# A two-layer fp32 decoder trunk on one core: norm tails moved to VectorE, softmax statistics moved to ScalarE's DMA queue, and a re-ordered start

## The chip, the cores and the metric

The kernel runs on one core of one Trainium2 chip. A core has five engines that run beside each other, each with its own in-order instruction stream: TensorE (PE; its weight loads are listed as PEld), VectorE (DVE), ScalarE (ACT), GpSimd (POOL) and SyncE (SP). Sixteen DMA engines move data. The metric is the device time of one launch in microseconds (us), the median of several runs. The profile is of one execution and has its own time.

## The reference

One sequence of 1024 positions, model width 1024, two layers, all fp32:

```python
for i in range(DEPTH):                       # DEPTH = 2
    j = i // N_MIXERS
    if i % N_MIXERS == 0:
        y = dilated_attention_mixer(x, attn_w_in[j], attn_w_out[j])
    else:
        y = hgrn2_mixer(x, hgrn_w_in[j], hgrn_w_out[j], hgrn_norm_g[j], lbs[i])
    x = layer_norm(DEEPNORM_ALPHA * x + y, ln_mix_g[i], ln_mix_b[i])
    y = squared_relu_mlp(x, ffn_w_up[i], ffn_w_down[i])     # width 4096
    x = layer_norm(DEEPNORM_ALPHA * x + y, ln_ffn_g[i], ln_ffn_b[i])
```

The attention has 16 heads of 64 and three dilations, 1, 4 and 16. Each query sees itself and the 128 keys behind it in its residue class. The three outputs of a head are mixed per position by a softmax over their log-sum-exps:

```python
for g, (window, dilation) in enumerate(((128, 1), (512, 4), (2048, 16))):
    o, lse = dilated_window_attention(rotary(q[g]), rotary(k[g]), v[g], window, dilation)
    outs.append(o); lses.append(lse)
wts = softmax(stack(lses), axis=0)
o = einsum('gbsh,gbshe->bshe', wts, stack(outs))  @ w_out
```

The second layer's mixer is a gated linear recurrence (HGRN2) of 8 heads of 128, computed in chunks of 64 positions, with a norm per head.

## The kernel before, in words

Every fp32 product is done as three matmuls on split operands: a value is cut into a high part in the format fp32r (a ScalarE copy) and a low part (a VectorE difference), and high x high, low x high and high x low are added in PSUM. `split` does the cut; its two lines appear in the profile as L137 (ScalarE) and L138 (VectorE).

**Attention, projections.** The input projection uses seven products of combined blocks instead of eight. `make_T(i)` forms the combined and split input block of product kind `i` (the blocks T1 to T4 are differences, L351); blocks are kept in DRAM (`keep_T`) and loaded again by `get_T` (L394). Weights are loaded by `load_w`, combined by VectorE (`wc`, L423 to L429), and split by `split_w_` (ScalarE, high half, L432) and `low_w` (VectorE, low half, L440) into a tile `H`. `product(n)` runs 12 matmuls of 128x512 (L669 to L671) for the product `n`; its result is copied by ScalarE or added by VectorE into `e`, `vp` and `vT` (L692 to L704). There are 12 groups of 21 products; a group serves two units, a unit being one pair of heads with one dilation, so there are 8 x 3 = 24 units.

**Attention, units.** The rest of a unit (rotary, scores L502, exponentials L516, transposes of the probabilities `ppt` L526, their copies `pts` L529, the products with v into bank `o` L541, and the copies `og` L549 and L552) is cut into pieces. They are put behind the products of the next group through the table `fill`.

**Mixing of the dilations.** For each unit `combine_tr` transposes the statistics, copies them to `sr` (ScalarE, L569), stores `sr` to the DRAM tensor `mdram` (L572), and loads it in another layout into `ml` (L578 for dilation 1, L581 for the others). After the third unit of a pair `combine` works out the weights `fh` and `fl` (high and low, L612 and L614) and writes them by six DMAs into the rows of `frow` (L619). `combine_mul` spreads them with a matmul into `fb` (L629) and multiplies and adds (L630 to L633). All DMAs of the kernel are issued by SP.

**The end of attention.** The last group's units have no products behind which they could stand; the lists `tail` and `mine` place their pieces between the matmuls of the output projection (`rows`, L183 to L185, with the split inputs `aoh`, `aol` and weights `woh`, `wol`).

**Norms.** `ln_math` (L193 to L214) makes the statistics on VectorE and ScalarE, subtracts the mean and multiplies by the gain in one VectorE pass (L199), scales by the inverse deviation on ScalarE (L213) and adds the bias on GpSimd (L214). The result `z` is transposed by TensorE (`lnpt`, L223) and split again (L233, L234) as input of the next part. The last norm of the kernel writes its output instead (L207 to L212).

**Feed-forward and recurrence.** `ffn` runs an up projection (L1116 to L1118) and a down projection (L1264 to L1268). `hgrn` runs the recurrence by heads: the pieces of head `hd` are put into a list `pend` that runs beside the projections of the next head (L171 to L173).

**Order.** The instructions of an engine run in the order of its stream. A scheduler sets that order, except where `in_order` pins a stretch to the order in which the code is written: TensorE and VectorE in attention; TensorE, VectorE and SP in the feed-forward part. ScalarE's order is the scheduler's everywhere.

Of the kernel before, what the change touches and what calls it, by code (L numbers as in the profile page):

```python
# [22 lines left out]
DIL = (1, 4, 16)  # L23
# [12 lines left out]
SPILL = (6, 5)  # L36
NKA = (6, 7)
EARLY = (2, 0)
NAHEAD = 8
NSTAY = 4  # L40
LATE = 2
# [21 lines left out]
def trunk_kernel(  # L63
# [62 lines left out]
    nc.scalar.preload_act_table_set("natural_log_exp_and_others")  # L126
    ident = cp.tile([P, P], F32, name="ident")
    make_identity(nc, ident)
    eps_ln = cp.tile([P, 1], F32, name="eps_ln")
    nc.gpsimd.memset(eps_ln, LN_EPS)  # L130
    eps_rms = cp.tile([P, 1], F32, name="eps_rms")
# [4 lines left out]
    def split(raw, hi, lo):  # L136
        act(hi, raw, AF.Copy)  # L137
        nc.vector.tensor_sub(lo, raw, hi.bitcast(F32))  # L138
# [54 lines left out]
    def ln_math(z, gB, bB, store=None):  # L193
        st = small([P, 2, 6], "lnst")
        for i in range(2):
            nc.vector.bn_stats(st[:, i], z[:, i * 512:(i + 1) * 512])
        mv = small([P, 2], "lnmv")
        nc.vector.bn_aggr(mv, st)
        nc.vector.scalar_tensor_tensor(z, z, mv[:, 0:1], gB, op0=ALU.subtract, op1=ALU.mult)  # L199
        w = small([P, 4], "lnw")  # L200
        act(w[:, 0:1], mv[:, 1:2], AF.Ln, bias=eps_ln)
        act(w[:, 1:2], w[:, 0:1], AF.Exp, scale=-0.5)
        r = w[:, 1:2]
        nc.vector.tensor_scalar(w[:, 2:3], mv[:, 1:2], LN_EPS, r, op0=ALU.add, op1=ALU.mult)
        nc.vector.tensor_scalar(w[:, 2:3], w[:, 2:3], r, -0.5, op0=ALU.mult, op1=ALU.mult)
        nc.vector.tensor_scalar(w[:, 3:4], w[:, 2:3], 1.5, r, op0=ALU.add, op1=ALU.mult)
# [6 lines left out]
        act(z, z, AF.Copy, scale=w[:, 3:4])  # L213
        nc.gpsimd.tensor_add(z, z, bB)  # L214

    def z_tr(z):

# [104 lines left out]
    def attention(pre, hc):  # L322
# [30 lines left out]
        def make_T(i):  # L353
            v, g = nc.vector, nc.gpsimd
            if i == 6:
                combine_x("T1", xr["12"], xr["11"], v)
                combine_x("T2", xr["22"], xc["T1"], v)
            elif i == 7:
                combine_x("T3", xr["22"], xr["12"], v)
            elif i == 4:  # L360
                combine_x("T4", xr["21"], xc["T2"], v)
            src = {1: "11", 2: "21", 6: "T2", 7: "T3", 3: "22", 5: "T1", 4: "T4"}[i]
            src = xc.pop(src) if src == "T3" or src == "T4" else xc[src] if src in xc else xr[src]
            hi = [U("xh", F32R) for _ in range(2)]
            lo = [U("xl", F32R) for _ in range(2)]
            for q in range(2):
                if i == 2:
                    for c in (L, R):
                        split(src[q][:, c], hi[q][:, c], lo[q][:, c])
                else:  # L370
                    split(src[q], hi[q], lo[q])
            return hi, lo
# [64 lines left out]
        def low_w(n):  # L437
            if n in lows:
                v = nc.vector
                v.tensor_sub(H[n][:, R], lows.pop(n), H[n][:, L].bitcast(F32))  # L440
# [123 lines left out]
        def combine_tr(pr, g, slot, ml):  # L564
            pt = bank("pt", "mpt")
            nc.tensor.transpose(pt[:, 0:P], allS, ident)
            q = slice(slot * 32, slot * 32 + 32)
            sr = small([P, P], "sr", 2)
            act(sr[q], pt[q, 0:P], AF.Copy)  # L569
            yield  # L570
            md = mdram[pr, g]
            nc.sync.dma_start(md.rearrange("w h (b q) -> (w h b) q", q=P), sr[q])  # L572
            yield

            d = DIL[g]
            for w in range(2):
                if d == 1:
                    nc.sync.dma_start(ml[:, w, 0, :], md[w].rearrange("h (i n) -> (h i) n", n=P))  # L578
                else:
                    for h in range(2):  # L580
                        nc.sync.dma_start(  # L581
                            ml[8 * h:8 * h + 8, w, g, :].rearrange("i (r n) -> i r n", r=d),
                            md[w, h].rearrange("(r i n) -> i r n", r=d, i=8))
            yield

        def combine(pr, ml):
# [27 lines left out]
            v.tensor_sub(fl, l, fh.bitcast(F32))  # L614
            yield
            for g in range(NG):
                for i, f in enumerate((fh, fl)):
                    r = 4 * g + 2 * i
                    nc.sync.dma_start(frow[r:r + 2, :].bitcast(F32).rearrange("h (i t) -> h i t", t=P),  # L619
                                      f[:, g, :].bitcast(F32))  # L620
            yield

        def combine_mul(pr, og, hb):
# [124 lines left out]
        for c in (R, L):  # L748
# [3 lines left out]
            if c == R:  # L752
                for q in range(2):
                    load_x("11", q)
        get_T(0, 0)
        for b in ("12", "22"):
            for q in range(2):
                load_x(b, q)
        for n in range(LOADW):
            load_w(n)  # L760
        for n in range(SPLITW):
            split_w_(n)
            if n <= SPLITW - 2:
                low_w(n)
        for n in range(len(seq)):
            gi, i, j = seq[n]
            load_w(n + LOADW)
# [14 lines left out]
            if n >= len(seq) - 2 * PREA - 1:  # L782
                next(early, None)
            if n == 0:
                get_T(2, 0)
            if n in KEEP:
                keep_T(KEEP[n])
            product(n)
            for f in fill.pop(n, []):
                f()  # L790
            low_w(n + SPLITW - 2)
            split_w_(n + SPLITW)
            if n % 21 == 14:
                last = gi == len(groups) - 1
                base = n + 7
# [25 lines left out]
        (ra, ca, sa, _), (rb, cb, sb_, mx) = tail  # L821
        done = [f for n in sorted(fill) for f in fill[n]]
        mine = [[ra[0]], [rb[0], rb[1]], [ra[1]], [ca[0], rb[2]], [ca[1]], [cb[0]], [ca[2]], [cb[1]], [ca[3]], [cb[2]],
                [ca[4]] + sa, [cb[3]], [ca[5]], [cb[4]] + sb_, [cb[5]], mx[:1], mx[1:3], mx[3:5], [],
                mx[5:7], mx[7:10], mx[10:]]
        lists = [done[k:k + 1] + (mine[k] if k < len(mine) else []) for k in range(max(len(done), len(mine)))]
        return oN, lists
# [661 lines left out]
    def hgrn(xs, late, consts, pre, gw):  # L1489
# [104 lines left out]
        for hd in range(8):  # L1594
# [64 lines left out]
            oN.append(ond[1, hd] if hd < SPILL[1] else oNt)  # L1659
            new = head_pieces(hd, cur["kd"], cur["kd2"], cur["qd"], e[2], cur["dec"], oNt)  # L1660
            if hd == 0:
                new = [[]] + new
            pend = [(pend[i] if i < len(pend) else []) + (new[i] if i < len(new) else [])
                    for i in range(max(len(new), len(pend)))]
        return oN, pend
# [98 lines left out]
```

## Time and profile before

| | |
|---|---|
| median of 3 runs | 2829.61 us (2828.23 to 2829.97) |
| the profiled execution's own time | 2828.98 us |
| its span, first to last instruction | 2827.2 us |
| TensorE, VectorE, ScalarE, GpSimd busy | 2766.7, 2069.0, 1450.8, 122.9 us |
| GpSimd in the norms' add (L214) | 24 instructions, 58.6 us |
| mean clock granted to TensorE | 0.997 |

The span is the time between the first and the last instruction on the core; the rest of the run's time lies around it. A row of the timeline gives the start, the duration, the engine, the line in the code, what is written from what, the shapes and, in brackets, how long the engine had been idle and what ended that wait. A row with "x2" holds two instructions in a row. In the rows of the waits, the numbers are the total, the count and the longest wait.

### The profile page before, as it was taken

To read this page: it belongs to the slowest core of one execution; us is meant where nothing else is said; L and a number is where in the kernel's file an instruction comes from. 1 tells how busy PE (TensorE), PEld (TensorE's weight loads), DVE (VectorE), ACT (ScalarE), POOL (GpSimd) and SP (SyncE) were. 2 spreads that over 40 slices of the span, in tenths; PEclk is the share of its full clock that TensorE was granted. 3 is DMA by queue.
4 is the path that set the end of the run, shared out by engine and by line. 5 is a ranking of instruction groups with operands and counts; after the bars stand their busy time and mean duration, and the time that the engine had idled before them with its cause. 6 is when DMAs were issued, how large, how long until landed. Compare 5 with 4: busy or idle time off the path is not lost.

```text
span 2827.2 us, 40131 instructions
## 1 busy us (share of the span) xinstructions
PE 2766.7 (98%) x14280; PEld 2229.3 (79%) x14280; DVE 2069.0 (73%) x3830; ACT 1450.8 (51%) x3105; POOL 122.9 (4%) x68
## 2 busy tenths in 40 slices
PE   8999999999999989999999999999999999999998
PEld 6777777777777757888878887788887788878887
DVE  7768777777877767786686876565667787678687
ACT  5455555655555555544454444555553644454443
POOL 0000000000000003100000011111102200000000
PEclk9999999999999999999999999999999999999999
DMA  7766665766666523464494752011132355475654
GB/s 286 255 187 208 191 207 173 217 201 198 201 200 220 168 83 134 146 224 160 152 324 127 260 178 98 8 60 60 61 112 104 128 211 176 154 278 188 221 176 130
DMA packets 204936, 485.27 MB, mean 172 GB/s; under 512 B 29376, under 2 KB 43712, under 8 KB 204736
## 3 DMA queue, kind: packets, MB, share of 16 engines
q1 hardware_dynamic: 204736, 482.72, 51.1%
q8 instruction: 112, 1.84, 0.3%
q14 instruction: 88, 0.72, 0.1%
HBM read 362.82 MB, written 94.24 MB: 162 GB/s over the span
## 4 chain that ended last, share of the span: by engine, by line
PE 90%; DVE 5%; ACT 2%; DMA 1%; issue 1%; POOL 0%; SPq 0%; DVEq 0%; POOLq 0%; ACTq 0%
PE pmm L669 8%; PE pmm L671 8%; PE pmm L670 8%; PE pup L1118 7%; PE pup L1116 7%; PE pup L1117 7%; PE pdy L1268 4%; PE pdy L1264 4%; PE pdy L1267 4%; PE s L502 3%; PE pdx L1267 3%; PE pmm L171 3%; PE pdx L1268 3%; PE pmm L173 3%; PE pdx L1264 3%; PE pmm L172 3%
## 5 line engine op out<-in xcount | busy, mean ns | idle before, releaser
L669 PE MATMUL pmm<-xh,H 128*128 128x512 f32 x1008 | 408.5, 405 | 13.2 <-ACT H L432 9.6
L671 PE MATMUL pmm<-xh,H 128*128 128x512 f32 x1008 | 396.5, 393 | 0.2 <-DVE H L440 0.2
L670 PE MATMUL pmm<-xl,H 128*128 128x512 f32 x1008 | 396.0, 393 | 0.0
L669 PEld LDWEIGHTS pmm<-xh,H 128*128 128x128 f32 x1008 | 190.8, 189 | 54.1 <-ACT H L432 9.6
L671 PEld LDWEIGHTS pmm<-xh,H 128*128 128x128 f32 x1008 | 190.4, 189 | 42.6 <-DVE H L440 1.1
L670 PEld LDWEIGHTS pmm<-xl,H 128*128 128x128 f32 x1008 | 191.1, 190 | 36.6
L516 ACT ACTIVATE p<-p,stats 128x128 f32<-128x128 f32 (+1 forms) x384 | 168.3, 441 | 90.7 <-DVE stats L513 89.3
L1264 PE MATMUL pdy<-dT,dS 128*128 128x512 f32 x512 | 199.2, 389 | 0.0
L1267 PE MATMUL pdy<-dT,dS 128*128 128x512 f32 x512 | 199.2, 389 | 0.0
L1268 PE MATMUL pdy<-dT,dS 128*128 128x512 f32 x512 | 199.2, 389 | 0.0
L513 DVE CUSTOM_DVE_ANT_0 p<-s,mask 128x128 f32<-128x128 f32 (+1 forms) x384 | 113.3, 348 | 66.5 <-PE s L502 56.8
L137 ACT ACTIVATE dS<-dr 128x512 fp32r<-128x512 f32 x192 | 119.5, 622 | 73.1 <-PE pdy L1268 36.6
L171 PE MATMUL pmm<-f0nh,wh 128*128 128x512 f32 x384 | 153.1, 399 | 0.0
L173 PE MATMUL pmm<-f0nh,wl 128*128 128x512 f32 x384 | 150.1, 391 | 1.7 <-DVE wl L138 1.6
L172 PE MATMUL pmm<-f0nl,wh 128*128 128x512 f32 x384 | 149.8, 390 | 0.0
L138 DVE TENSOR_TENSOR dS<-dr,dS 128x512 fp32r<-128x512 f32 x192 | 135.4, 705 | 16.2 <-ACT dS L137 14.3
L214 POOL TENSOR_TENSOR z<-z,bB 128x1024 f32<-128x1024 f32 x24 | 58.6, 2444 | 1673.1 <-ACT z L213 1663.0
L529 ACT ACTIVATE pts<-ppt 128x256 f32<-128x256 f32 (+1 forms) x192 | 85.4, 474 | 61.1 <-PE ppt L526 59.0
L137 ACT ACTIVATE dT<-hold 128x512 fp32r<-128x512 f32 x128 | 80.0, 625 | 69.0 <-DVE hold L1243 28.4
L1077 ACT ACTIVATE H<-wc 128x512 fp32r<-128x512 f32 x128 | 77.2, 625 | 73.3 <-DVE wc L1070 43.9
L1267 PEld LDWEIGHTS pdy<-dT,dS 128*128 128x128 f32 x512 | 96.1, 188 | 20.0
L1268 PEld LDWEIGHTS pdy<-dT,dS 128*128 128x128 f32 x512 | 96.1, 188 | 20.0
(396 smaller groups left out, 6946.6 us busy)
## 6 DMA issues: line engine op xcount, KB each, us to landing
xh<-xtd SPq DMA_DIRECT2D x110, 512.0 KB
xl<-xtd SPq DMA_DIRECT2D x110, 512.0 KB
dr<-hd SPq DMA_DIRECT2D x192, 256.0 KB
dr<-in_w_down_dram SPq DMA_DIRECT2D x128, 256.0 KB
rot<-e SPq DMA_DIRECT2D x192, 128.0 KB
wa<-in_w_up_dram SPq DMA_DIRECT2D x48, 512.0 KB
wb<-in_w_attn_dram SPq DMA_DIRECT2D x36, 512.0 KB
wa<-in_w_attn_dram SPq DMA_DIRECT2D x33, 512.0 KB
```

The source lines that it names most:

```text
L137: act(hi, raw, AF.Copy)
L171: nc.tensor.matmul(o, wh[:, k], xs.h(k), start=k == 0, stop=False)
L172: nc.tensor.matmul(o, wh[:, k], xs.l(k), start=False, stop=False)
L173: nc.tensor.matmul(o, wl[:, k], xs.h(k), start=False, stop=k == NK - 1)
L669: nc.tensor.matmul(o, wh, hi[k // 2][:, c], start=begin and k == 0, stop=False, skip_group_check=True)
L670: nc.tensor.matmul(o, wh, lo[k // 2][:, c], start=False, stop=False, skip_group_check=True)
L671: nc.tensor.matmul(o, wl, hi[k // 2][:, c], start=False, stop=end and k == 3, skip_group_check=True)
L1116: nc.tensor.matmul(o, wh, xf.h(b, k), start=begin and k == 0, stop=False, skip_group_check=True)
L1117: nc.tensor.matmul(o, wh, xf.l(b, k), start=False, stop=False, skip_group_check=True)
L1264: nc.tensor.matmul(o[q], h, T_[:, L], start=begin, stop=False, skip_group_check=True)
L1267: nc.tensor.matmul(o[q], h, T_[:, R], start=False, stop=False, skip_group_check=True)
L1268: nc.tensor.matmul(o[q], l, T_[:, L], start=False, stop=end, skip_group_check=True)
```

## The change

1. **Norms.** The ScalarE pass L213 and the GpSimd add L214 become one VectorE instruction, 24 times.
2. **Statistics.** The store `mdram <- sr` is issued on ScalarE's queue. For dilation 1 there is no trip through DRAM: two DMAs on ScalarE's queue copy `sr` to `ml` directly. Of the six `frow` DMAs of a pair, the three of `fh` go to ScalarE's queue. So ScalarE issues 56 DMAs: 24 for `frow`, 16 stores to `mdram` and 16 direct copies to `ml`.
3. **Last units.** In `mine` the statistics are transposed one slot sooner than they are used.
4. **Warm-up.** 24 transposes of the identity with no use are put at TensorE's start.
5. **Start.** Weight 0 is split between the two halves of the first input block; weights 1 to 5 are split ahead of the next block; a table `FIRSTW` puts off the splits that follow.
6. **First output.** ScalarE follows the written order from product 30 to 33.
7. **Recurrence.** Head 0's pieces start one slot later.

The diff, cut where a part only renames:

```diff
+FIRSTW = {0: (), 1: (), 2: (), 3: ((0, 6),), 4: ((0, 7), (1, 6)), 5: ((0, 8), (1, 7), (0, 9), (1, 8)),
+          6: ((1, 9), (0, 10), (0, 11))}
+NWARM = 24
+FIRSTO = (30, 34)
...
+    warm = bank("s", "warm")
+    for n in range(NWARM):
+        nc.tensor.transpose(warm[:, n % 4 * P:(n % 4 + 1) * P], ident, ident)
...
-        act(z, z, AF.Copy, scale=w[:, 3:4])
-        nc.gpsimd.tensor_add(z, z, bB)
+        nc.vector.scalar_tensor_tensor(z, z, w[:, 3:4], bB, op0=ALU.mult, op1=ALU.add)
...
                 if i == 2:
                     for c in (L, R):
                         split(src[q][:, c], hi[q][:, c], lo[q][:, c])
+                    if q == 0:
+                        between()
...
-            nc.sync.dma_start(md.rearrange("w h (b q) -> (w h b) q", q=P), sr[q])
+            d = DIL[g]
+            if d == 1:
+                for w in range(2):
+                    nc.scalar.dma_start(ml[:, w, 0, :], sr[q0 + 16 * w:q0 + 16 * w + 16])
+            else:
+                nc.scalar.dma_start(md.rearrange("w h (b q) -> (w h b) q", q=P), sr[q0:q0 + 32])
...
-                for i, f in enumerate((fh, fl)):
+                for i, (f, eng) in enumerate(((fh, nc.scalar), (fl, nc.sync))):
...
-        get_T(0, 0)
...
-        for n in range(SPLITW):
+        opT[0] = make_T(2, lambda: (split_w_(0), low_w(0)))
+        for n in range(1, 6):
             split_w_(n)
-            if n <= SPLITW - 2:
-                low_w(n)
+            low_w(n)
+        acts = in_order((mybir.EngineType.Activation,))
...
             if n == 0:
-                get_T(2, 0)
+                combine_T(6)
+            if n == FIRSTO[0]:
+                acts.__enter__()
+            if n == FIRSTO[1]:
+                acts.__exit__()
...
-            low_w(n + SPLITW - 2)
-            split_w_(n + SPLITW)
+            if n in FIRSTW:
+                for f, m in FIRSTW[n]:
+                    (split_w_, low_w)[f](m)
+            else:
+                low_w(n + SPLITW - 2)
+                split_w_(n + SPLITW)
...
-                [ca[4]] + sa, [cb[3]], [ca[5]], [cb[4]] + sb_, [cb[5]], mx[:1], mx[1:3], mx[3:5], [],
+                [ca[4]] + sa[:1], sa[1:] + [cb[3]], [ca[5]], sb_[:1] + [cb[4]], sb_[1:] + [cb[5]], mx[:1], mx[1:3], mx[3:5], [],
...
             if hd == 0:
-                new = [[]] + new
+                new = [[], []] + new
```

How the streams move, at three places. A row is a position in the engine's stream, the line, the operation and what is written from what; line numbers of the changed code are 12 to 14 higher in attention.

VectorE at the start, before. `xl` is the low part of an input block (the full blocks 112 and 114 are those of the second block, xT_171 and xT_172 the block T2), `H` the low half of a weight, `wc` a combined weight:

```order
3 L440 TENSOR_TENSOR H<-wa,H 128x512 x4
4 L138 TENSOR_TENSOR xl<-x_112,xh 128x1024
5 L138 TENSOR_TENSOR xl<-x_114,xh 128x1024
10 L138 TENSOR_TENSOR xl<-xT_171,xh 128x1024
11 L138 TENSOR_TENSOR xl<-xT_172,xh 128x1024
12 L440 TENSOR_TENSOR H<-wa,H 128x512
13 L423 TENSOR_TENSOR wc<-wb 128x512
14 L424 TENSOR_TENSOR wc<-wc,wa 128x512
15 L440 TENSOR_TENSOR H<-wa,H 128x512
16 L423 TENSOR_TENSOR wc<-wb 128x512
```

And after the change:

```order
2 L452 TENSOR_TENSOR H<-wa,H 128x512
3 L145 TENSOR_TENSOR xl<-x_130,xh 128x512 x2
4 L452 TENSOR_TENSOR H<-wa,H 128x512 x5
5 L145 TENSOR_TENSOR xl<-x_137,xh 128x1024
6 L145 TENSOR_TENSOR xl<-x_139,xh 128x1024
11 L145 TENSOR_TENSOR xl<-xT_200,xh 128x1024
12 L145 TENSOR_TENSOR xl<-xT_201,xh 128x1024
13 L708 TENSOR_TENSOR e<-pmm,e 128x512
14 L435 TENSOR_TENSOR wc<-wb 128x512
15 L436 TENSOR_TENSOR wc<-wc,wa 128x512
```

The low halves of weights 4 and 5 moved from behind the blocks T2 to the front, and weight 0's into the middle of the first block.

ScalarE at the first output, before; `og` is the copy of the finished bank `o`, `p,stats` the exponentials:

```order
62 L457 ACTIVATE bsel<-selw 128x384
63 L529 ACTIVATE pts<-ppt 128x256 x2
64 L516 ACTIVATE p,stats<-p,stats 128x128 x4
65 L698 ACTIVATE vp<-pmm 128x512
66 L700 ACTIVATE e<-pmm 128x512
67 L698 ACTIVATE e<-pmm 128x512
68 L552 ACTIVATE og<-o 128x8x64
```

And after:

```order
61 L469 ACTIVATE bsel<-selw 128x384
62 L712 ACTIVATE e<-pmm 128x512
63 L564 ACTIVATE og<-o 128x8x64
64 L528 ACTIVATE p,stats<-p,stats 128x128 x4
65 L541 ACTIVATE pts<-ppt 128x256 x2
66 L444 ACTIVATE H<-wc 128x512
67 L712 ACTIVATE vp<-pmm 128x512
```

The copy `og` moved ahead of the exponentials, the copies `pts` and two copies of projections.

ScalarE at the end of attention, before, where no DMA stands in its stream:

```order
778 L599 ACTIVATE ml<-ml 16x384
779 L137 ACTIVATE aoh<-og 128x512
780 L137 ACTIVATE aoh<-onr 128x512 x2
781 L612 ACTIVATE fh<-ml 16x384
782 L137 ACTIVATE aoh<-onr 128x512
783 L137 ACTIVATE aoh<-og 128x512 x3
```

And after:

```order
821 L613 ACTIVATE ml<-ml 16x384
822 L144 ACTIVATE aoh<-onr 128x512
823 L144 ACTIVATE aoh<-og 128x512
824 L144 ACTIVATE aoh<-onr 128x512
825 L626 ACTIVATE fh<-ml 16x384
826 L633 DMA frow<-fh 2x8x128 x3
827 L144 ACTIVATE aoh<-onr 128x512
828 L144 ACTIVATE aoh<-og 128x512
```

Three issues of `frow` now stand between `fh` and the next split of the projection's input.

More of the change, by code (lines that the diff above doesn't have):

```diff
@@ L351, in combine_x, with combine_T @@
                 eng.tensor_sub(xc[name][q], x[q], y[q])
-        def make_T(i):
-            v, g = nc.vector, nc.gpsimd
+        def combine_T(i):
+            v = nc.vector
             if i == 6:
@@ L361, in make_T @@
                 combine_x("T4", xr["21"], xc["T2"], v)
+        def make_T(i, between=None):
+            if i != 6:
+                combine_T(i)
             src = {1: "11", 2: "21", 6: "T2", 7: "T3", 3: "22", 5: "T1", 4: "T4"}[i]
@@ L566, in combine_tr @@
             nc.tensor.transpose(pt[:, 0:P], allS, ident)
-            q = slice(slot * 32, slot * 32 + 32)
+            q0 = slot * 32
             sr = small([P, P], "sr", 2)
-            act(sr[q], pt[q, 0:P], AF.Copy)
+            act(sr[q0:q0 + 32], pt[q0:q0 + 32, 0:P], AF.Copy)
             yield
             md = mdram[pr, g]
-            nc.sync.dma_start(md.rearrange("w h (b q) -> (w h b) q", q=P), sr[q])
-            yield
[L575 to L579, printed above, removed]
+            d = DIL[g]
[4 more added lines that the diff above has]
+                nc.scalar.dma_start(md.rearrange("w h (b q) -> (w h b) q", q=P), sr[q0:q0 + 32])
+            yield
+            if d > 1:
+                for w in range(2):
                     for h in range(2):
@@ L616, in combine @@
             for g in range(NG):
-                for i, f in enumerate((fh, fl)):
+                for i, (f, eng) in enumerate(((fh, nc.scalar), (fl, nc.sync))):
                     r = 4 * g + 2 * i
-                    nc.sync.dma_start(frow[r:r + 2, :].bitcast(F32).rearrange("h (i t) -> h i t", t=P),
-                                      f[:, g, :].bitcast(F32))
+                    eng.dma_start(frow[r:r + 2, :].bitcast(F32).rearrange("h (i t) -> h i t", t=P),
+                                  f[:, g, :].bitcast(F32))
             yield
```

## The prediction

> **What bounds the kernel now.** I read the engine shares of the page first, then the waits of TensorE (PE), then short pieces of the timeline at the longest of them. The page's engine lines:
>
> ```profile
> PE 2766.7 (98%) x14280; PEld 2229.3 (79%) x14280; DVE 2069.0 (73%) x3830; ACT 1450.8 (51%) x3105; POOL 122.9 (4%) x68
> ```
>
> The reader is to see that TensorE works for 2766.7 of 2827.2 us. Its matmuls are the same after the change, so only its 60.5 us of idle time, and the time in which it works at half clock, can be won. The view of waits says which instruction TensorE waited for (total, times, longest):
>
> ```profile
> PE pmm L669 <- ACT H L432: 9.6, 1, 9.6
> PE pmm L183 <- ACT aoh L137: 4.9, 3, 3.6
> PE pmm L669 <- ACT e L692: 3.6, 1, 3.6
> PE o L541 <- ACT og L552: 3.0, 3, 2.1
> PE fb L629 <- DMA frow<-fh: 2.5, 1, 2.5
> PE lnpt L223 <- issue: 2.3, 3, 1.0
> PE lnpt L223 <- DVE f0nl L234: 2.1, 1, 2.1
> PE pmm L173 <- DVE wl L138: 1.6, 1, 1.6
> PE as L1515 <- DVE qe L1654: 1.4, 1, 1.4
> PE ho L1553 <- DVE stA L1535: 1.3, 1, 1.3
> ```
>
> These ten rows hold 32.3 us, and the change reaches for every one of them. The first three and the clock belong to the start. In the stretches below, the engine columns are busy us and (instructions), then the granted clock.
>
> ```profile
> 9.60:14.10 4.50, 4.50 (x11) 3.43 (x12) 2.38 (x5) 2.04 (x4) 0.00 (x0) 1.00 1.04 406
> 24.40:27.80 3.40, 3.40 (x10) 2.66 (x9) 3.33 (x7) 1.47 (x3) 0.00 (x0) 0.50 1.02 407
> 120.00:123.30 3.30, 3.30 (x10) 2.53 (x9) 0.00 (x0) 1.57 (x4) 0.00 (x0) 0.50 0.77 313
> 23.80:49.80 26.00, 26.00 (x108) 21.38 (x109) 24.84 (x33) 13.86 (x22) 0.00 (x0) 0.93 0.47 184
> ```
>
> A half-clock stretch shows as 10 matmuls in 3.4 us (0.34 us each with the edges; 0.41 in the first row) where 108 in 26.0 us is 0.24 each. Each costs about 1.1 to 2.0 us: 10 x (0.34 - 0.24) = 1.0 at the least, half of 3.4 = 1.7 if the whole stretch is at half. I take 1.7. The first row's clock column reads 1.00, but its 11 matmuls in 4.5 us say half: 11 x (0.41 - 0.23) = 2.0 us lost.
>
> **Part A: warm-up transposes, weight 0 in halves, splits of weights 1 to 5 ahead.** The matmul that waits longest could start before 9.58, but what stands behind it decides the gain: VectorE (DVE).
>
> ```profile
> 1.22 0.29 POOL masks.py:199 TENSOR_SCALAR_AFFINE_SELECT ident<-ident 128x128 f32<-128x128 f32 x1
> L526 PE MATMUL ppt<-ident,p x4: 272/273/327, 96.0 to 96.4; 128*128 128x128 f32 x4
> 15.27 2.36 DVE L138 TENSOR_TENSOR xl<-x,xh 128x1024 fp32r<-128x1024 f32 x2 [0.93 <-ACT xh L137]
> 33.89 1.09 DVE L694 TENSOR_TENSOR vT<-pmm,vp 128x512 f32<-128x512 f32 x1 [0.83 <-PE pmm L671]
> 49.09 0.69 DVE L440 TENSOR_TENSOR H<-wb,H 128x512 fp32r<-128x512 f32 x1
> 50.46 0.39 PE L671 MATMUL pmm<-xh,H 128*128 128x512 f32 x1
> ```
>
> The identity is ready at 1.5 us. Four warm transposes start within 0.4 us, 0.13 each, so 24 at half clock take 24 x 0.26 = 6.2 us and end near 7.8. TensorE was idle until 9.58, so they cost nothing, unless weight 0 is there earlier than 7.8; the first product then starts some 1.8 us sooner. At full clock from there it saves the 2.0 of the first stretch. The wait for e (3.6 us) halves, because the copy of e now stands ahead of the two xh copies of T2 instead of behind them, and its cold stretch of 1.7 goes. Together 1.8 + 2.0 + 1.8 + 1.7 = 7.3 us if TensorE alone decided.
>
> VectorE does not allow it. From 23.8 to 49.8 it is busy 24.84 of 26.00 us, and the low half of weight 12, made from 49.09 to 49.78, is read at 50.46: slack 0.7. VectorE's work to that point is the same after the change. What it gains: two low halves (H4, H5; about 0.6 each at their pitch) go ahead of xl into its idle time, 1.2; the idle 0.83 at 33.89 goes; against it, its first full xl waits for a ScalarE that splits H5 first, so it starts near 15.8 instead of 15.27, -0.5. With the slack, 0.7 + 1.2 + 0.8 - 0.5 = **2.2 us** is how much earlier TensorE can pass that weight. I take 2.2, since the busy share says that VectorE is the bound; ends: 0 (the splits collide with late loads) and 7.3.
>
> **Part B: ScalarE in written order at the first output.**
>
> ```profile
> 109.34 0.66 PE L541 MATMUL o<-pts,vn 128*64 128x128 f32 x8
> 116.76 0.60 ACT L700 ACTIVATE e<-pmm 128x512 f32<-128x512 f32 x1 [2.12 <-PE pmm L671]
> 117.73 1.03 ACT L552 ACTIVATE og<-o 128x512 f32<-128x512 f32 x1
> 118.81 0.66 PE L541 MATMUL o<-pts,vn 128*64 128x128 f32 x8 [2.09 <-ACT og L552]
> ```
>
> The o bank is complete at 110.0, but ScalarE copies it at 117.73, behind copies of e for which it waits on TensorE itself. In the new order one copy of e is left ahead of og, of the product two before the one that 116.76 waits for: 116.76 - 2 x 12 x 0.23 = 111.2. So og is done near 113, the wait of 2.09 goes, and so does the half-clock stretch from 120.0 behind it, 1.7: **3.8 us**. Ends: -1 (an exponential pushed back by og, 1.03) and 3.8. Late next are the exponentials, four at 0.4 as they always were, read by transposes well behind.
>
> **Part C: statistics on ScalarE's queue.** Rows at the end of attention, then the price of an issue on SP (min/median/max ns):
>
> ```profile
> 1040.81 0.61 ACT L137 ACTIVATE aoh<-og 128x512 fp32r<-128x512 f32 x1
> 1045.75 0.62 SPq L619 DMA_DIRECT2D frow<-fh  x1
> 1051.98 1.19 PE L629 MATMUL fb<-frow,bsel 128*128 128x512 f32 x2 [2.46 <-DMA frow<-fh]
> L619 SPq DMA_DIRECT2D frow<-fh x24: 610/623/712, 242.7 to 1049.2; - x24
> L619 SPq DMA_DIRECT2D frow<-fl x24: 610/611/645, 250.0 to 1049.8; - x24
> L572 SPq DMA_DIRECT2D mdram<-sr x24: 317/328/338, 125.2 to 1033.5; - x24
> L578 SPq DMA_DIRECT2D ml<-mdram x16: 312/392/509, 208.4 to 1035.4; - x16
> ```
>
> Six frow issues follow one another on SP from 1045.75 to 1050.4; the last lands about 1.5 later, and fb starts at 1051.98. With three on each queue the last is issued near 1048.6, which saves 1.8. For dilation 1 the trip through DRAM goes: one issue (0.33) and one landing (1.5); half of that lies beside waits for other loads, so I take 1.0. Together **2.8 us**. The clock stays half there, since most of the 3.6 us wait for aoh stays. Ends: -1.9 (three issues of 0.62 ahead of the aoh copies on ScalarE) and 4.2 (the whole 2.5 and a cold stretch of 1.7).
>
> DMA: Bandwidth & Descriptors in the Trainium skill, section "Issuing engines are not separate DMA queues", says that all queues run on the same engines and that a second issuer saves issue time alone. By it the term would be 1.8 and the sum 1.0 less; dropping a trip is outside that rule, so I stay with 2.8.
>
> The cost: 56 DMAs now stand in ScalarE's in-order stream, 24 frow x 0.62 + 16 mdram x 0.33 + 16 ml x 0.39 = 26.4 us, over the eight pairs of heads. No row shows an issue on ScalarE. Ends: 0 (hidden; ScalarE is busy 51%) and -26.4 (each delays a split or an og that TensorE reads). Nearest to the first end: in attention the waits list has only one og and one e above 1 us. I take **-1.5**.
>
> **Part D: norms on VectorE, head 0 of the recurrence later.**
>
> ```profile
> L213 ACT ACTIVATE z<-z,lnw 128x1024 f32<-128x1024 f32 x24 | 27.6, 1150 | 25.3 <-DVE lnw L206 25.2
> L214 POOL TENSOR_TENSOR z<-z,bB 128x1024 f32<-128x1024 f32 x24 | 58.6, 2444 | 1673.1 <-ACT z L213 1663.0
> 1729.70 1.28 DVE L199 SCALAR_TENSOR_TENSOR z<-z,lnmv,gB 128x1024 f32<-128x1024 f32 x1
> 1720.59 0.41 DVE L138 TENSOR_TENSOR d3s<-d,d3s 128x256 fp32r<-128x256 f32 x1
> 1722.34 4.75 POOL L214 TENSOR_TENSOR z<-z,bB 128x1024 f32<-128x1024 f32 x2 [47.42 <-ACT z L213]
> 1724.82 2.89 DVE L138 TENSOR_TENSOR d3s<-d,d3s 128x256 fp32r<-128x256 f32 x2
> ```
>
> Per norm 1.15 + 2.44 us of ScalarE and GpSimd become one VectorE pass of the form of L199, 1.28, so the row is ready 2.3 us sooner; the three transposes that wait for issue (2.3) are also placed some 20 matmuls later: 2.0 of it. The f0nl wait (2.1) stands behind a VectorE held beside GpSimd, and a pass now lands among its pieces: 1.0. The wl wait (1.6): 1.2. That is 4.2. VectorE gets 24 x 1.2 = 28.8 us of new work at 73% busy; for the halves that TensorE already waits on narrowly I take -1.5 (ends: +2, as below, and -28.8).
>
> Two d3s differences at 0.41 took 2.89 us beside the GpSimd add: each such meeting costs VectorE about 2 us, and the adds go. SBUF — State Buffer in the Trainium skill, "Who interferes with whom", calls it an exclusive lock against an operation with two SBUF inputs; the trace agrees (2.89). By it up to 24 x 2 us of holds would return, the -1.5 would be 0, and the sum 1.5 more; I keep -1.5, as most meetings lie where TensorE has slack.
>
> Head 0 of the recurrence a slot later takes the qe and stA waits, 2.7, less 0.4 for the step that moves into the gap: **2.3** (ends -0.5 and 3.0).
>
> **Sum.** 2.2 + 3.8 + 2.8 - 1.5 + 4.2 - 1.5 + 2.3 = 12.3 us against the profiled execution's 2828.98: 2816.7. The median of the runs stands 0.6 above that execution, so **2817.3 us**. About 0.2%, 5.7 us, is what a measurement of this kernel can tell from no change.
>
> **The rivals.**
> - *ScalarE's queue becomes the bound in attention (other side).* An issue waits for its data and for its lane, and every split, copy and og behind it waits too. All 26.4 exposed instead of 1.5 gives 2817.3 + 24.9 = 2842; half, 2829. It decides from 13.8 / 56 = 0.25 us per DMA, where the gain is gone, and from 19.5 / 56 = 0.35 the kernel is slower beyond the bound. For it: issues of 0.62 back to back; against it: ScalarE is half idle. Chance 0.17: 0.03 still faster, 0.08 same, 0.06 slower.
> - *The start is TensorE's, not VectorE's.* All 7.3 comes: 2812.2. Against it, 24.84 of 26.00. Chance 0.08.
> - *VectorE cannot carry the norms.* The 4.2 is not won and another 1.5 is lost: 2823.0. For it, 28.8 us of added work where differences of operands already set waits. Chance 0.10, of which 0.05 counts as no change.
> - *The order at the first output does not do what it says.* Pinned, ScalarE waits for something else written ahead of og; 3.8 stays: 2821.1. Chance 0.10.
>
> My forecast has the remaining 0.55 (alone 2812 to 2822). Faster 0.55 + 0.03 + 0.08 + 0.05 + 0.10 = 0.81, same 0.13, slower 0.06. The range runs from 2809, below the early start with larger terms in C, to 2829, half of the issue cost.
>
> **What would show it.** A right: the first product near 7.8, no wait of 3.6 for e, but waits for H of VectorE at products 6 to 12. B right: no og wait near 118 and full clock from 120. C right: fb near 1049, less what came earlier; wrong: new waits for ACT e, og or H between 200 and 1000. D right: no GpSimd add, lnpt without waits for issue, and d3s pairs of 0.8; wrong: new waits for VectorE in the feed-forward parts. Most of all I would be wrong if ScalarE's issues took longer than SP's.

## The result, and the profile after

The changed kernel takes 2818.3 us (median of 6 runs, 2816.39 to 2820.14); the kernel before took 2828.66 us in its 6 runs. The ratio is 0.9962, with a 95% interval of 0.9952 to 0.9973: faster by 0.38%. The forecast was 2817.3 us, in a range of 2809 to 2829. The total came out 1.0 us from the forecast, but its terms did not: several are wrong by more than that, and they cancel.

The profiled execution took 2820.14 us, the slowest of the six, with a span of 2818.4 us. Its engine line on the page:

```profile
PE 2771.4 (98%) x14304; PEld 2235.1 (79%) x14304; DVE 2067.9 (73%) x3854; ACT 1425.7 (51%) x3081; POOL 65.4 (2%) x44
```

GpSimd lost 57.5 us. VectorE got 24 instructions more and is busy 1.1 us less than before, which will matter below. TensorE's longest waits now:

```profile
PE pmm L190 <- ACT aoh L144: 4.9, 1, 4.9
PE ho L1570 <- DVE stB L1557: 3.5, 2, 3.2
...
PE hpt L1529 <- ACT vn L1530: 2.5, 1, 2.5
...
PE pmm L685 <- DVE H L452: 2.0, 3, 1.1
PE pmm L683 <- ACT H L444: 2.0, 1, 2.0
...
PE pmm L683 <- ACT e L706: 1.6, 1, 1.6
...
PE lnpt L229 <- DVE f0nl L240: 1.4, 1, 1.4
...
PE o L553 <- ACT og L564: 0.8, 2, 0.6
```

The waits for frow, for issue at the transposes, for wl, qe and stA are gone. At head 0 of the recurrence the wait for vn is new and the one for stB has grown from 0.4 to 3.5 us. The wait for aoh is now one of 4.9, where the longest of three was 3.6.

To see where the time went, I paired the matmuls of the two traces, the n-th of a line in one with the n-th of the same line in the other, and took the difference of their starts. This is the lead of one kernel over the other at that place of the program (medians over 8 us; place in us of the kernel before):

| place | 30 | 60 | 100 | 130 | 900 | 990 | 1065 | 1115 | 1250 | 1700 | 1765 | 1785-1870 | 2140 | 2200 | 2700 |
|---|---|---|---|---|---|---|---|---|---|---|---|---|---|---|---|
| changed over before | 7.4 | 0.6 | 0.4 | 4.1 | 4.6 | 6.3 | 5.2 | 6.6 | 6.3 | 6.3 | 10.8 | falls to 5.9 | 5.9 | 8.1 | 8.4 |

The last 0.4 us of the 8.8 between the two spans lie behind the last place. A step that the change makes repeats in other kernels with the same step, and this was used as the finer measure: the runs of one kernel differ by up to 7 us among themselves, while a step of the lead that the edit makes comes again to within some tenths. A stretch at half clock is no such step: it can come in one execution and not in another, and 3.4 us of it cost 1.7. In the kernel with part 1 alone one at 987 us, where its code is that of the kernel before, takes 1.7 us of its lead.

### The profile page after: what moved, and what is told of

Same layout as the page of the kernel before. It is cut to its first block, busy times and chain, and to the rows that moved or that the text cites. A ratio compares the mean times of both kernels' runs of the same rounds, so it can differ in the third digit from the quotient of the medians.

```text
span 2818.4 us, 40019 instructions
## 1 busy us (share of the span) xinstructions
PE 2771.4 (98%) x14304; PEld 2235.1 (79%) x14304; DVE 2067.9 (73%) x3854; ACT 1425.7 (51%) x3081; POOL 65.4 (2%) x44
## 5 line engine op out<-in xcount | busy, mean ns | idle before, releaser
L145 DVE TENSOR_TENSOR dS<-dr,dS 128x512 fp32r<-128x512 f32 x192 | 131.0, 682 | 15.2 <-ACT dS L144 15.2
L1286 PEld LDWEIGHTS pdy<-dT,dS 128*128 128x128 f32 x512 | 96.1, 188 | 20.1
L1289 PEld LDWEIGHTS pdy<-dT,dS 128*128 128x128 f32 x512 | 96.1, 188 | 19.9
L1290 PEld LDWEIGHTS pdy<-dT,dS 128*128 128x128 f32 x512 | 96.1, 188 | 19.9
```

The costliest lines, as they stand in the source:

```text
L1286: nc.tensor.matmul(o[q], h, T_[:, L], start=begin, stop=False, skip_group_check=True)
L1289: nc.tensor.matmul(o[q], h, T_[:, R], start=False, stop=False, skip_group_check=True)
L1290: nc.tensor.matmul(o[q], l, T_[:, L], start=False, stop=end, skip_group_check=True)
```

## The experiments

Each block gives the edit, what was expected of it, and what came. The kernel before was run beside each; its medians were 2828.5 to 2829.5 us.

**Without the later slot of head 0** (from the changed kernel):

```diff
-                new = [[], []] + new
+                new = [[]] + new
```

> The changed kernel without its part 7: head 0 of the recurrence starts in its old slot. Theory S (the later slot itself costs): the changed kernel was 10.8 us ahead of the kernel before at 1780 us and only 5.9 ahead at 1860; without the shift the lead stays near 10.8, and the time is 2818.3 - 4.9 = 2813.4 us, with the old short waits for qe and stA (1.4 and 1.3) in place of 2.5 for vn and 3.2 for stB. Rival N (VectorE's new norm pass collides with head 0 wherever it stands): the lead still falls to about 6, 2818 us. The prediction as recorded (the shift is worth 2.3): 2820.6 us.

2813.82 us (5 runs), ratio 0.9946 (0.9934 to 0.9959). The lead over the changed kernel is 0.4 us at 1765 and 5.3 to 5.4 from 1870 to the end: 4.9 us of it come at head 0. Theory S held, and the old short waits came back with it, as this kernel's list of waits says:

```profile
PE as L1537 <- DVE qe L1676: 1.4, 1, 1.4
PE ho L1575 <- DVE stA L1557: 1.3, 1, 1.3
```

ScalarE's rows of the changed kernel show what the shift did:

```profile
1788.05 1.15 ACT L1651 ACTIVATE a<-ls,hc_CA 128x1024 f32<-128x1024 f32 x1 [2.61 <-DVE ze L1650]
...
1791.48 1.14 ACT L1653 ACTIVATE a<-a,one 128x1024 f32<-128x1024 f32 x1
1792.52 1.07 ACT L1530 ACTIVATE vn<-hpt 128x512 f32<-128x512 f32 x2
```

and TensorE's and VectorE's, behind it:

```profile
1793.15 1.14 PE L1529 MATMUL hpt<-ident,ze 128*128 128x128 f32 x8 [2.50 <-ACT vn L1530]
1811.34 1.23 DVE L1676 TENSOR_TENSOR qe<-qe,a 128x1024 f32<-128x1024 f32 x1 [1.10 <-ACT a L1675]
1814.96 0.44 PE L1570 MATMUL ho<-vn,aT 128*64 128x128 f32 x4 [3.15 <-DVE stB L1557]
```

A slot later, the copies vn of head 0 stand behind the gates of the next head (L1645 to L1653) in ScalarE's stream, which itself waits 2.6 us for VectorE at 1788. Without the shift the copy stands ahead of them:

```profile
1781.59 0.59 ACT L1530 ACTIVATE vn<-hpt 128x512 f32<-128x512 f32 x1
```

That row is from the kernel without the shift. The chain of states stB likewise got the next head's qe, and the wait in front of it, between its links. The clock fell behind the second wait (0.76 of full speed, third number from the end; the kernel before and the one without the shift have 1.00 in the same stretch):

```profile
1815.00:1822.00 7.00, 7.00 (x47) 5.85 (x48) 3.51 (x9) 1.01 (x3) 0.00 (x0) 0.76 0.01 2
```

That is the account of the shift: 3.0 us of old waits go (1.36 + 1.28 + 0.36, as in the kernel before), 2.50 + 3.15 + 0.34 = 6.0 come, and 0.24 x 7.0 = 1.7 are lost to the clock: 4.7 of the 4.9. All five traces with the later slot have a half-clock stretch behind that wait. Of the nine without it two have one near 1800 (the two with ScalarE in written order from product 0), so such a stretch can come there without the shift too.

**The later slot alone** (the kernel before with that one line):

> The kernel before with part 7 alone. Theory S: TensorE waits for vn and stB between 1790 and 1825, 4.9 us are lost: 2828.7 + 4.9 = 2833.6 us, if the shift collides by itself. If it collides only because the changed kernel arrives at head 0 in another rhythm (rival R), the old waits of 2.7 go and little comes: 2826 to 2829 us.

2832.11 us (11 runs), ratio 1.0010 (1.0001 to 1.0019), 2.7 us slower. The time lies between theory S and rival R; the trace decides it: the lead over the kernel before is 1.4 us at 1785 and -3.5 from 1870 on, a loss of 4.9 us at the same place with the same two waits (vn 2.5, stB 3.2). The 1.4 us ahead are differences between two executions of the same code: 0.7 from the start on, 0.7 in small steps after it.

**The norms alone** (the kernel before with part 1):

```diff
-        act(z, z, AF.Copy, scale=w[:, 3:4])
-        nc.gpsimd.tensor_add(z, z, bB)
+        nc.vector.scalar_tensor_tensor(z, z, w[:, 3:4], bB, op0=ALU.mult, op1=ALU.add)
```

> The kernel before with part 1 alone (norm tail on VectorE). Theory: the trace of the changed kernel gains 4.5 us between 1720 and 1752, 2.2 between 2160 and 2190 and about 1.4 between 1060 and 1100, 0.3 is lost or gained elsewhere; alone it gives 2828.7 - 8.1 = 2820.6 us, so that the norms are the largest term (4.2 less 1.5 was predicted). Rival (VectorE cannot carry 28.8 us more): 2827 to 2831 us.

2821.43 us (6 runs), ratio 0.9971 (0.9959 to 0.9982), 8.0 us faster. The lead rises by 1.4 us from 1065 to 1115, by 4.6 between 1700 and 1765 and by 2.2 between 2140 and 2200: 8.2 in all, and the changed kernel has the same three steps (1.4, 4.5, 2.2). The 1.7 us of clock at 987, named above, are the main reason why its trace ends only 6.3 ahead. The norms are the largest term of the change.

**Without the idle transposes** (the changed kernel with NWARM's loop left out):

> The changed kernel without the 24 idle transposes. Theory (VectorE is the bound of the start): the first three products run at half clock again, the lead near 30 us falls from 7.4 to about 5, but the lead at 60 us stays 0.6 within 0.3, and the time stays 2818.3 within 1. Rival (TensorE's own clock bounds the start): 2 to 3.5 us slower, 2820.3 to 2821.8 us.

2819.22 us (5 runs), ratio 0.9965 (0.9952 to 0.9977). At 10 us it is 0.7 us behind the changed kernel, at 30 us 0.7 ahead, at 60 us 0.1 ahead. The end of the expectation held, its middle did not: I had expected it to be 2.4 us behind at 30 us, and VectorE already binds there. In this kernel the first three matmuls start at 6.71, 7.31 and 7.74 at half clock, and it costs nothing that can be measured. At the end its trace is 1.9 behind; 1.5 of that come near 2337 us, far from the edit, and their cause is open.

**The first output alone** (the kernel before with ScalarE in written order for products 30 to 33):

```diff
+            if n == 30:
+                acts.__enter__()
+            if n == 34:
+                acts.__exit__()
```

> The kernel before with part 6 alone (ScalarE in written order from product 30 to 33). Theory: the wait for og at 118.8 (2.1) and the half-clock stretch from 119.8 behind it (1.7) go, nothing else moves: 2829.5 - 3.7 = 2825.8 us, and the lead over the kernel before steps from 0 to 3.7 at 119 us. Rival (in the changed kernel it was the earlier start that brought og forward): 2829 us.

2826.29 us (11 runs), ratio 0.9989 (0.9980 to 0.9998), 2.8 us faster by the medians. The lead steps from 2.13 us to 5.84 at 119 us: 3.7, as expected. Over the rest it varies by 2 us, to 4.5 at the end; the 2.13 is the start, whose code is the same in both. The kernel before has a half-clock stretch from 24.4 to 27.8 us that this execution has not. Two executions of the same start can differ by that much.

**ScalarE in written order from product 0** (the changed kernel without the shift, FIRSTO from 0):

> The changed kernel without part 7, and with ScalarE in written order from product 0 instead of 30. In the changed kernel VectorE stands idle 1.0 us at 38.8, because the second xh of the block T3 lies behind a copy of e in ScalarE's stream. Theory (that idle is the missing part of term A): the lead at 60 us rises from 0.6 to about 1.5, 2813.8 - 0.9 = 2812.9 us. Rival (the written order puts other splits behind copies that wait for TensorE): the lead at 60 us falls, 2814 to 2817 us.

2813.07 us (5 runs), ratio 0.9943 (0.9929 to 0.9956). The lead over the kernel without the shift is 0.4 us at 60 us where 0.9 was expected; the idle 1.0 us of VectorE at 38.8 is gone, and a similar one (0.97) stands at 50.9. A lead of 0.4 is within what two executions of one start differ by, so neither the theory nor the rival is shown. At the end the two are not to be told apart.

**Statistics on SP again** (the changed kernel; every scalar-queue issue of part 2 goes to SP, the direct copies for dilation 1 stay):

> The changed kernel with all statistics DMAs issued by SP again; the direct copies for dilation 1 stay. Theory (the issues on ScalarE cost nothing in attention and the queue is worth little at its end, by the trace 0.4 up to 970 us, and 1.8 less 1.1 from there to 1060): 2818.3 + 1.1 = 2819.4 us. Rival of the prediction (ScalarE's queue costs up to 26.4 us exposed): faster, 2816 us or less. The recorded term C without its cost (2.8): 2821.1 us.

2820.61 us (6 runs), ratio 0.9971 (0.9959 to 0.9982). Its median is 2.3 us above that of the changed kernel, but the runs overlap (2817.2 to 2824.2), and in the trace it falls by 1.8 us at 979 of the changed kernel, to 1.2 behind, and is level at 1065 and at the end (within 0.4). So the queue is worth at most what the runs cannot tell, and the rival of a costly queue is out.

**Parts 2 and 3 taken back altogether** (from the changed kernel):

> The changed kernel with parts 2 and 3 taken back altogether: every statistics DMA on SP, the trip through DRAM for dilation 1 too, and the transposes of the last statistics in their old slots. The lead over the changed kernel is the size of term C. Theory (worth little: in the trace of the changed kernel 0.4 up to 970 us, and 1.8 less 1.1 from there to 1065): -1.1 us at 1065, 2819.4 us. Term C as recorded with its cost (2.8 - 1.5): -1.3, and without it (2.8): -2.8, 2821.1 us. Rival (with SP alone the wait for frow and the old half clock are no worse than what the changed kernel has there): 0 within 0.4, 2818.3 us.

2819.84 us (5 runs), ratio 0.9964 (0.9951 to 0.9978). In the trace it is level at 900, 1.8 us behind at 980, 0.3 at 1065, 0.5 at the end. Between the small theory and the rival: term C is 0.3 to 0.7 us.

**The difference of T3 on GpSimd** (the changed kernel without the shift):

```diff
-                combine_x("T3", xr["22"], xr["12"], v)
+                combine_x("T3", xr["22"], xr["12"], nc.gpsimd)
```

> The changed kernel without part 7, and with the two differences of the block T3 (2.35 us of VectorE at 34 us) made by GpSimd. Theory V (VectorE's amount of work bounds the start): VectorE passes weight 12 up to 2.3 us sooner, the lead at 60 us rises from 0.6 to between 1.5 and 2.5, 2811.9 to 2812.9 us. Rival L (GpSimd holds VectorE while both read, as it did at 1724 us in the kernel before, where two operations of 0.41 took 2.89): VectorE loses 2 us per GpSimd operation, the lead at 60 us is 0 or negative, 2814 to 2816 us.

2818.48 us (5 runs), ratio 0.9963 (0.9950 to 0.9975), 4.7 us slower than without that edit; the lead over that kernel is -4.4 at 30 us, -4.0 from 60 us on, and stays near it. Rival L held, and more strongly than expected. This kernel's rows, two subtractions in each:

```profile
17.56 6.73 POOL L357 TENSOR_TENSOR xT<-x,x 128x1024 f32<-128x1024 f32 x2 [16.05 <-DMA x<-in_xT_dram]
17.49 4.55 DVE L357 TENSOR_TENSOR xT<-x,x 128x1024 f32<-128x1024 f32 x2
21.96 4.55 DVE L357 TENSOR_TENSOR xT<-x,xT 128x1024 f32<-128x1024 f32 x2
```

VectorE's pairs took 2.35 us each in the changed kernel (at 18.82 and 21.09); beside GpSimd they took 4.55. That is 2.2 us lost for each of the two GpSimd instructions, close to the 2.1 that the prediction's pair of d3s lost to one. GpSimd's pair took 6.73, where one instruction of that size took 2.4 in the norms of the kernel before. VectorE lost 4.4 us here and TensorE 4.0 at 60 us, so with that work on it VectorE's chain sets the time of the start. What follows for the start is that VectorE cannot be relieved in this way.

**Without the difference of T3** (the changed kernel without the shift; block 22 stands in for T3):

```diff
-                combine_x("T3", xr["22"], xr["12"], v)
+                xc["T3"] = list(xr["22"])
```

> The changed kernel without part 7, with the two differences of the block T3 left out (block 22 stands in for T3, so one product kind works on other data). That takes 2.35 us of work off VectorE at 34 us and gives it to nobody. Theory V (VectorE's amount of work bounds the start): the lead over the run without part 7 is 1.5 to 2.3 us at 60 us and stays, about 2811.9 us. Rival (TensorE, ScalarE or the loads bound it): within 0.4 of 0, 2813.8 us.

2813.35 us (4 runs), ratio 0.9945 (0.9931 to 0.9959). The lead over the kernel without the shift is 1.6 us at 60 us and holds to 740, as theory V has it; by itself it is no proof, since two executions of one start differ by up to 2.1. It did not reach the end: at 753 this execution has a wait of 1.8 us for a low half of a weight that is not in the other traces. VectorE stood 7.6 us there for a load of rot, 4.1 in the kernel without the shift; why the load came late is open.

**Idle transposes at the end of attention** (the changed kernel without the shift; 36 transposes right ahead of the matmul that waits for aoh):

```diff
+                if hot and k == ks[-1]:
...
+                    for m in range(NHEAT):
+                        nc.tensor.transpose(warm2[:, m % 4 * P:(m % 4 + 1) * P], ident, ident)
```

> The changed kernel without part 7, with 36 idle transposes of the identity put into TensorE's stream right ahead of the matmul that waits 4.9 us for aoh at 1036. In the changed kernel 12 matmuls at 1039 to 1044 and 6 at 1051 to 1054 ran at half clock. Theory G (the half clock behind the wait is what ate the gain of the earlier frow): the first 12 run at full clock, 12 x 0.2 = 2.4 us less, 2813.8 - 2.4 = 2811.4 us, and the lead over the run without part 7 is 1.5 to 2.4 us from 1065 on. Rival Q (behind it TensorE waits for VectorE's and the DMAs' chain to og and aol anyway): the lead at 1065 is within 0.5 of 0, 2813.8 us.

In the trace theory G holds: the lead over the kernel without the shift goes from 0.85 at 1020 to 2.4 at 1065, 1.5 us. The stretches of the changed kernel, and then of this one, with the granted clock as the third number from the end (the kernel without the shift has 0.50 and 0.51 in the first two):

```profile
1039.20:1044.40 5.20, 5.20 (x14) 4.05 (x13) 2.60 (x5) 1.67 (x3) 0.00 (x0) 0.50 0.05 13
1051.50:1054.10 2.60, 2.60 (x8) 2.00 (x7) 2.60 (x6) 0.00 (x0) 0.00 (x0) 0.50 0.02 6
```

```profile
1035.20:1044.40 9.20, 7.05 (x26) 4.54 (x26) 5.47 (x11) 2.15 (x4) 0.00 (x0) 1.00 0.14 46
1044.40:1054.10 9.70, 6.67 (x23) 3.99 (x23) 9.69 (x17) 1.89 (x3) 0.00 (x0) 1.00 0.48 151
```

The measured time does not follow: 2816.12 us (5 runs, 2812.9 to 2818.1), ratio 0.9954 (0.9942 to 0.9967), 2.3 above the kernel without the shift, whose interval overlaps with it. The profiled execution was its fastest run; the others were not profiled. Their mean granted clock was 0.996 to 0.998, that of the profiled one 0.998; 0.001 of the span is 2.8 us, so part of the difference can lie in half-clock stretches at places that no trace shows. The half clock is shown as the cause in one execution, and no gain in time is shown.

**All that helped** (without the shift, order from product 0, transposes at the end of attention):

> All that has helped: the changed kernel without part 7, ScalarE in written order from product 0, and the 36 idle transposes at the end of attention. By theory G 2813.1 - 2.4 = 2810.7 us; by rival Q 2813.1 us.

2813.13 us (5 runs), ratio 0.9945 (0.9931 to 0.9959): rival Q's figure. It is no better than the single edit of the first experiment. The versions that beat both kernels, 2813 to 2814 us, have one thing in common: head 0 in its old slot.

## Why the prediction was right, and where it was not

| term | predicted | measured | from |
|---|---|---|---|
| A, start | 2.2 | 0.4 (0.3 to 1.9) | lead at 60 to 100 us, five kernels with this start |
| B, first output | 3.8 | 3.7 | lead at 119 us, also alone |
| C, statistics | 2.8 | 0.3 to 0.7 | lead from 900 to 1065; parts taken back |
| issues on ScalarE | -1.5 | 0 (+0.4) | lead from 130 to 900 |
| D, norms | 4.2 - 1.5 = 2.7 | 8.0 | part 1 alone |
| head 0 later | 2.3 | -4.9 | part 7 alone and taken back |

Term B was right in mechanism and size: og is copied at 109.75 and the 120 matmuls between 110 and 130 run without a break at full clock.

```profile
109.75 1.04 ACT L564 ACTIVATE og<-o 128x512 f32<-128x512 f32 x1
110.00:130.00 20.00, 20.00 (x120) 15.24 (x118) 12.68 (x53) 13.87 (x39) 0.00 (x0) 1.00 0.72 274
```

It came earlier than I had worked out (113), since the copy of e that I put ahead of it did not hold it.

Term A was right in mechanism as far as the experiments tell: VectorE bounds the start. TensorE was 7.4 us ahead at 30 us, which is the 7.3 that I gave for a start bounded by TensorE alone, and had lost all but 0.6 by 60 us. The 7.3 is in part luck: its terms were 1.8 + 2.0 + 1.8 + 1.7, and the lead grew by 3.0 with the first product (at 6.60, not near 7.8), 1.0 by its half clock, 1.9 at the wait for e and 1.5 by the half clock behind that. Nor did half clock go from the start: a stretch from 30.8 to 34.2 us took the place of the one at 24.4. (The wait for aoh, which the prediction counts among those of the start, lies at the end of attention.) The size of the VectorE sum was wrong. These rows of the changed kernel tell by what, in this execution:

```profile
16.54 2.36 DVE L145 TENSOR_TENSOR xl<-x,xh 128x1024 fp32r<-128x1024 f32 x2 [0.26 <-ACT xh L144]
38.82 1.23 DVE L145 TENSOR_TENSOR xl<-xT,xh 128x1024 fp32r<-128x1024 f32 x1 [1.01 <-ACT xh L144]
49.03 0.69 DVE L452 TENSOR_TENSOR H<-wb,H 128x512 fp32r<-128x512 f32 x1
49.77 0.50 PE L685 MATMUL pmm<-xh,H 128*128 128x512 f32 x1 [0.56 <-DVE H L452]
```

The first full xl starts at 16.54 where I had 15.8: 0.7. VectorE then waits 1.0 at 38.8 for a ScalarE copy that stands behind e. 2.2 - 0.7 - 1.0 = 0.5. The low half of weight 12 is ready 0.06 us earlier than before (49.03 against 49.09), and TensorE takes it 0.69 earlier (49.77 against 50.46), all of it the old slack. The wait of 1.0 comes again in the other kernels with this start (1.0 to 1.4), the late xl does not always (15.2 to 16.5). Against the same trace of the kernel before, the five kernels with the new start are 0.3 to 1.9 us ahead at 60 us, and three others with the old start 0.5 to 2.1. So the start has no gain that these traces can tell from nothing.

Term C failed at the step "the last frow lands sooner, and fb with it". The wait for frow did go: fb now starts at 1046.29, right behind the matmul ahead of it. But what was won came at another place, at a wait that I had not priced. In the kernel before, three loads of x into z stand behind an issue of frow in SP's stream; VectorE's sum z waits for them, and TensorE for z:

```profile
979.93 0.68 SPq L619 DMA_DIRECT2D frow<-fh  x1
980.71 1.29 SPq L911 DMA_DIRECT2D z<-in_x_dram  x3
984.39 0.69 DVE L937 SCALAR_TENSOR_TENSOR z<-z,pmm 128x512 f32<-128x512 f32 x1 [2.64 <-DMA z<-in_x_dram]
985.13 0.50 PE L183 MATMUL pmm<-woh,aoh 128*128 128x512 f32 x1 [1.51 <-DVE z L937]
```

In the changed kernel the loads are issued at 959.09, TensorE does not wait there, and the lead rises by 1.8. In both kernels with the statistics on SP the loads are issued at 975.5 and 976.2, and the wait is back (1.6 and 1.5). The changed kernel then lost 1.1 of it, since TensorE stood elsewhere:

```profile
1034.66 0.52 ACT L613 ACTIVATE ml<-ml 16x384 f32<-16x384 f32 x1 [4.55 <-DVE ml L612]
1036.27 0.79 PE L190 MATMUL pmm<-woh,aoh 128*128 128x512 f32 x1 [4.88 <-ACT aoh L144]
1046.63 0.63 ACT L144 ACTIVATE aoh<-onr 128x512 fp32r<-128x512 f32 x1 [3.46 <-DMA onr<-ond]
```

An exponential of the mixing stands ahead of aoh in ScalarE's stream and waits 4.55 us for VectorE; TensorE idles 4.9 us, and some 14 and 8 matmuls behind that run at half clock, against 9 and 7 there before. With parts 2 and 3 taken back the wait is 3.7, near the old 3.6. The last load onr waits on SP behind frow. I had said that the clock would stay half, at the old price. Both sums that I gave for the term, 2.8 and 1.8, were too high.

The cost of ScalarE's issues was bounded well and taken too high. An issue of frow or mdram takes about what it took on SP, one of ml more (0.58 against 0.39, but now from sr and not from DRAM; min/median/max ns):

```profile
L633 ACTq DMA_DIRECT2D frow<-fh x24: 617/659/1196, 237.9 to 1041.4; - x24
L589 ACTq DMA_DIRECT2D mdram<-sr x16: 308/316/366, 121.1 to 1019.3; - x16
L587 ACTq DMA_DIRECT2D ml<-sr x16: 533/581/711, 202.8 to 1025.4; - x16
```

24 x 0.66 + 16 x 0.32 + 16 x 0.58 = 30.2 us in ScalarE's stream, and the lead does not fall between 130 and 900 us. The rival on the other side is out.

Of the norms, the mechanism was right and the size was not. The pass costs what L199's form did, and holds beside GpSimd went, but I subtracted 1.5 for VectorE's load where its load hardly rose. Two rows of the kernel before and three of the changed kernel:

```profile
L199 DVE SCALAR_TENSOR_TENSOR z<-z,lnmv,gB 128x1024 f32<-128x1024 f32 x32 | 48.7, 1522 | 0.5
L138 DVE TENSOR_TENSOR d3s<-d,d3s 128x256 fp32r<-128x256 f32 x64 | 30.4, 478 | 11.3 <-ACT d3s L137 10.7
```

```profile
L220 DVE SCALAR_TENSOR_TENSOR z<-z,lnw,bB 128x1024 f32<-128x1024 f32 x24 | 30.6, 1276 | 0.1
L206 DVE SCALAR_TENSOR_TENSOR z<-z,lnmv,gB 128x1024 f32<-128x1024 f32 x32 | 40.9, 1279 | 0.4
L145 DVE TENSOR_TENSOR d3s<-d,d3s 128x256 fp32r<-128x256 f32 x64 | 26.6, 418 | 11.2 <-ACT d3s L144 10.7
```

And the engine line of the kernel with part 1 alone:

```profile
PE 2768.3 (98%) x14280; PEld 2231.1 (79%) x14280; DVE 2073.8 (74%) x3854; ACT 1425.4 (51%) x3081; POOL 64.4 (2%) x44
```

24 new passes are 30.6 us (not 28.8, as the prediction's 24 x 1.2 had it). With part 1 alone VectorE is busy 4.8 us more, so the rest of its work took 25.9 us less. The forms of L199 and of d3s, whose means are the same there as in the changed kernel within 2 ns, give 11.6 of that (32 x 0.243 + 64 x 0.060). The changed kernel is busy 1.1 us less than before, but other parts are in that figure. The Trainium skill's lock (SBUF — State Buffer, "Who interferes with whom") is borne out by this and by the T3 experiment, and its version of the sum, 1.5 more, was nearer. Between 1700 and 1765, 4.5 us came where I had 2.2: the wait for d3s at 1727 (1.25) I had not priced, and of the one for wl (1.57) only a part. The waits for issue at the transposes gave 3.6 where I had 2.0.

The step that failed outright is head 0. I priced the waits that go (qe, stA) and 0.4 for the step that fills the gap, and did not ask what each of the moved copies would stand behind on ScalarE and VectorE. The waits for qe and stA went, as forecast; what came in their place was twice as long and took the clock with it.

So the total was near because the norms gave 5.3 us more than forecast and head 0 took 7.2 more, with 1.8 and 2.1 to 2.5 missing at A and C and 1.5 to 1.9 not paid on ScalarE's queue. The measured terms add up to about 8.1 us, against 8.8 between the two profiled executions. The medians are 10.4 apart, in part because the one profiled of the changed kernel was its slowest; no term accounts for the other 2.3. That the forecast of 12.3 came so near to the medians is luck.

## What to carry to other kernels

When a step is moved to a later slot, list for each of its instructions what stands ahead of it in its engine's stream there, and what that waits for; the gap that it fills is the smaller half of the price. Where two engines hold each other up, count the holds that go as work taken off the engine that takes over: here 30.6 us of new work raised its busy time by 4.8. When a DMA's issue leaves a queue, list what stood behind it in that queue: here loads that had nothing to do with it gave the 1.8 us. An early start is worth only as much as the second engine's chain lets through: 7.4 us at 30 us were 0.6 at 60.

## What the runs showed of the hardware

GpSimd subtractions of 128x1024 beside VectorE's doubled VectorE's time (2.35 to 4.55 us for a pair), 2.2 us for each GpSimd instruction. Two executions of one and the same start differed by up to 2.1 us at 60 us, and the runs of one kernel here spread over 0.9 to 7.0 us; half-clock stretches do not sit at the same places in all traces. At the start of the kernel before, matmuls are 0.43 us apart from 9.58 to 14.0 us; in the kernel with the first output alone, whose start is the same, from 9.06 to 14.8. TensorE: Matmul & The Clock Gate in the Trainium skill, "The HAM clock gate", says that the window of the gate runs free of the kernel's start; these traces agree.
